# Both half-step ffns of a hybrid diffusion layer: from three token blocks to two token halves, with seven block products for gate, up and down

## The chip, the cores and the metric

One NeuronCore of a Trainium2 chip runs the whole kernel. The metric is the device time of one execution in microseconds; the kernel before takes 2794.5 us, the median of three runs (2792.1 to 2797.2). PE is TensorE, DVE VectorE, ACT ScalarE, POOL GpSimd; SP is the engine whose queue issues most DMAs.

## The reference

One layer for 1024 latent and 128 prompt tokens, each kind with its own conditioning vector. The change concerns the two ffns:

```
m = silu(cvec) @ ada_w + ada_b          # nine vectors of 1024: shift, scale, gate for three steps
x += 1/2 * gate1 * swiglu(modulate(rms_norm(x, ffn1_norm), shift1, scale1), w_gu, w_down)
x += gate2 * merge(attention A, attention B)
x += 1/2 * gate3 * swiglu(modulate(rms_norm(x, ffn2_norm), shift3, scale3), w_gu, w_down)
y = rms_norm(x, final_norm)
swiglu(h) = (silu(a) * u) @ w_down,   [a, u] = h @ w_gu
```

The model width is 1024, the hidden width 2816, all in float32.

## The kernel before

Activations lie transposed: width on 128 partitions times KD = 8, tokens along the row. The T = 1152 tokens make three blocks of BW = 384. The hidden width makes NF = 22 units j of 128; unit j has 128 gate and 128 up columns. Every float32 operand is split into a high and a low part (`split`: ACT casts, L175; DVE or POOL subtracts, L176), and one product of float32 is three matmuls (`mm3`: high weight by high activation L204, high by low L205, low by high L206). Weights come by DMA into `raw` and are split into `whi` and `wlo`.

Gate and up of an ordinary block take 2 x 8 x 3 = 48 matmuls per unit (`gu`). Blocks 1 and 2 are taken as a pair (`gu_pair`, L519): the two blocks by two halves of the width are a 2 by 2 matrix of activations, gate and up by two halves of the width a 2 by 2 matrix of weights, and their product is formed by seven block products with sums and differences in place of eight. `norm_pair` (L467) builds the sums of activations (tiles t0 to t2), POOL four combinations of the weights per unit (L543). That makes 48 + 84 = 132 matmuls of 384 columns per unit. Down (`down`, L437) is plain, in groups of two or three units, 22 x 8 x 3 x 3 = 1584 matmuls, each result scaled and added to x by DVE (`upd`, L414). Hidden activations stay in SBUF.

What follows in PE's stream is the order in which generators yield: the main program (`ffn`, L596) runs, and at every yield `step` lets side jobs take turns at a rate of so many per yield (`spawn`). Side jobs are the normalizations (`self.cm`), and the rest of the modulation vectors (`ada_rest`, L767, rates AR = (2, 0.4)): the first two are made before anything else (L747), the other seven in four groups as matmuls of 512 columns (L256) among the products. `need_gate` and `finish` run a side job to its end where its result is needed. A tile's buffer is filled again only when its last reader is done, and each engine runs its instructions in order, as does SP its DMAs.

## Time and profile before

| | |
|---|---|
| median of 3 runs | 2794.5 us |
| the profiled execution | 2805.29 us, 10.8 above the median |
| its span, first to last instruction | 2803.2 us |
| mean granted clock of TensorE | 0.979 |
| instructions | 39143 |
| DMA | 290.46 MB, mean 104 GB/s |

A row of the page or of a view names a line, an engine, an operation, the tile written and the tiles read, with shapes (partitions x columns); busy is the time of such instructions, and idle before is time in which their engine had nothing to do just ahead of them, with what ended it. The busy time of PE counts a stretch of overlapping matmuls once, so the distance between matmuls is read from starts, or from a count in a stretch that is busy throughout.

### The profile page before, as it was taken

To read this page: it belongs to the slowest core of one execution; us is meant where nothing else is said; L and a number is where in the kernel's file an instruction comes from. 1 tells how busy PE (TensorE), PEld (TensorE's weight loads), DVE (VectorE), ACT (ScalarE), POOL (GpSimd) and SP (SyncE) were. 2 spreads that over 40 slices of the span, in tenths; PEclk is the share of its full clock that TensorE was granted. 3 is DMA by queue.
4 is the path that set the end of the run, shared out by engine and by line. 5 is a ranking of instruction groups with operands and counts; after the bars stand their busy time and mean duration, and the time that the engine had idled before them with its cause. 6 is when DMAs were issued, how large, how long until landed. Compare 5 with 4: busy or idle time off the path is not lost.

```text
span 2803.2 us, 39143 instructions
## 1 busy us (share of the span) xinstructions
PE 2684.7 (96%) x15049; PEld 2505.1 (89%) x15049; DVE 1811.5 (65%) x2867; ACT 1049.0 (37%) x1636; POOL 762.0 (27%) x523
## 2 busy tenths in 40 slices
PE   7899999999999998899999989899999999999998
PEld 5699999999999998788877777789999999999998
DVE  3765555555687656566677777557676655555676
ACT  4522222222344533355555455235542222222333
POOL 2421111111233101244345444233331111111232
PEclk9999999999999999899999999999999999999997
DMA  7543332111214465433323233684421111111213
GB/s 264 173 130 104 108 111 83 46 46 46 99 45 158 139 206 164 112 86 90 91 72 102 77 97 116 192 281 150 128 78 44 45 46 46 46 46 46 76 53 106
DMA packets 161968, 290.46 MB, mean 104 GB/s; under 512 B 20206, under 2 KB 114914, under 8 KB 158454
## 3 DMA queue, kind: packets, MB, share of 16 engines
q1 hardware_dynamic: 160054, 283.24, 32.1%
q10 hardware_dynamic: 1728, 4.72, 0.4%
q8 instruction: 119, 1.95, 0.3%
q14 instruction: 67, 0.55, 0.1%
HBM read 233.77 MB, written 53.99 MB: 103 GB/s over the span
## 4 chain that ended last, share of the span: by engine, by line
PE 45%; DVE 6%; ACT 4%; issue 2%; DMA 2%; POOL 1%; SPq 0%; DVEq 0%; ACTq 0%; POOLq 0%
PE ps_g L206 7%; PE ps_g L204 7%; PE ps_g L205 7%; PE pp_m L205 3%; PE pp_m L204 3%; PE pp_m L206 3%; DVE pl L1298 3%; PE pp_o L204 1%; PE pp_o L205 1%; PE pp_o L206 1%; ACT ph L1297 1%; PE pp_o L1242 1%; ACT pf L1296 1%; PE pp_m L1213 1%; PE pp_o L1241 1%
## 5 line engine op out<-in xcount | busy, mean ns | idle before, releaser
L204 PE MATMUL ps_g<-hh,whi 128*128 128x384 f32 x1284 | 437.7, 342 | 11.7 <-ACT whi L175 6.1
L206 PE MATMUL ps_g<-hh,wlo 128*128 128x384 f32 x1284 | 436.3, 340 | 5.8 <-DVE wlo L176 5.8
L205 PE MATMUL ps_g<-hl,whi 128*128 128x384 f32 x1284 | 436.6, 340 | 1.8 <-DVE hl L176 1.8
L543 POOL TENSOR_TENSOR adaw<-adaw 128x512 f32<-128x512 f32 x132 | 181.7, 1376 | 813.3 <-DVE wlo L176 784.2
L176 DVE TENSOR_TENSOR wlo<-raw,whi 128x1024 fp32r<-128x1024 f32 (+1 forms) x203 | 261.5, 1289 | 167.3 <-ACT whi L175 167.0
L175 ACT CAST whi<-raw 128x1024 fp32r<-128x1024 f32 (+1 forms) x203 | 209.5, 1033 | 400.0 <-PE ps_g L205 215.1
L1305 POOL TENSOR_TENSOR acc<-acc,pf 128x1024 f32<-128x1024 f32 (+3 forms) x128 | 235.1, 1842 | 378.3 <-ACT pf L1296 271.6
L175 ACT CAST whi<-adaw 128x1024 fp32r<-128x1024 f32 x132 | 138.9, 1052 | 449.4 <-PE ps_g L205 310.4
L204 PEld LDWEIGHTS ps_g<-hh,whi 128*128 128x128 f32 x1284 | 245.4, 191 | 19.2 <-ACT whi L175 7.4
L206 PEld LDWEIGHTS ps_g<-hh,wlo 128*128 128x128 f32 x1284 | 245.4, 191 | 12.2 <-DVE wlo L176 9.1
L205 PEld LDWEIGHTS ps_g<-hl,whi 128*128 128x128 f32 x1284 | 245.8, 191 | 6.6 <-DVE hl L176 3.0
L204 PE MATMUL pp_m<-hh,whi 128*128 128x384 f32 x732 | 249.0, 340 | 1.8 <-ACT whi L175 1.3
L205 PE MATMUL pp_m<-hl,whi 128*128 128x384 f32 x732 | 249.8, 341 | 0.0
L206 PE MATMUL pp_m<-hh,wlo 128*128 128x384 f32 x732 | 249.1, 341 | 0.0
L176 DVE TENSOR_TENSOR wlo<-adaw,whi 128x1024 fp32r<-128x1024 f32 x132 | 170.4, 1291 | 106.2 <-ACT whi L175 105.9
L206 PE MATMUL ps_g<-ah,wlo 128*128 128x384 f32 x682 | 229.9, 337 | 2.3 <-DVE wlo L176 2.3
L204 PE MATMUL ps_g<-ah,whi 128*128 128x384 f32 x682 | 231.2, 339 | 0.0
L205 PE MATMUL ps_g<-al,whi 128*128 128x384 f32 x682 | 229.6, 337 | 0.0
L1298 DVE TENSOR_TENSOR pl<-pf,ph 128x1024 fp32r<-128x1024 f32 (+1 forms) x96 | 170.4, 1779 | 68.2 <-ACT ph L1297 65.9
L414 DVE SCALAR_TENSOR_TENSOR y<-ps_g,gate,y 128x384 f32<-128x384 f32 (+2 forms) x271 | 127.2, 503 | 42.4 <-PE ps_g L206 42.0
L204 PEld LDWEIGHTS pp_m<-hh,whi 128*128 128x128 f32 x732 | 139.4, 190 | 8.5 <-ACT whi L175 1.6
L205 PEld LDWEIGHTS pp_m<-hl,whi 128*128 128x128 f32 x732 | 139.5, 191 | 7.2 <-issue 2.7
(486 smaller groups left out, 6180.4 us busy)
## 6 DMA issues: line engine op xcount, KB each, us to landing
adaw<-gu SPq DMA_DIRECT2D x66, 512.0 KB
raw<-wd SPq DMA_DIRECT2D x52, 512.0 KB
adaw<-ada_w SPq DMA_DIRECT2D x24, 1024.0 KB
raw<-gu SPq DMA_DIRECT2D x46, 512.0 KB
raw<-win SPq DMA_DIRECT2D x27, 512.0 KB
raw<-wout SPq DMA_DIRECT2D x24, 512.0 KB
raw<-wo SPq DMA_DIRECT2D x16, 512.0 KB
gate_sp<-tmp SPq DMA_DIRECT2D x41, 192.0 KB
```

Of the source, the lines that this page charges most:

```text
L175: self.nc.scalar.copy(hi, src)
L176: (eng or self.nc.vector).tensor_sub(lo, src, hi.bitcast(F32))
L204: nc.tensor.matmul(ps, wh[:, c], mh, start=(start and i == 0), stop=False)
L205: nc.tensor.matmul(ps, wh[:, c], ml, start=False, stop=False)
L206: self.mm = nc.tensor.matmul(ps, wl[:, c], mh, start=False, stop=(stop and i == n - 1))
L414: nc.vector.scalar_tensor_tensor(x[:, d, c0:c1], ps[:, c0:c1], gate[:, d, c:c + 1], x[:, d, c0:c1], op0=ALU.mult, op1=ALU.add)
L543: nc.gpsimd.tensor_tensor(o, x, y, op=op)
L1213: nc.tensor.matmul(ps, q1[0:96, t * P:(t + 1) * P], k1[0:96, c0:c1], start=True, stop=True)
L1241: nc.tensor.matmul(out, V(kt), ph[:, i, :q1 - q0], start=(first[hf] == (n, i)), stop=False)
L1242: nc.tensor.matmul(out, V(kt), pl[:, i, :q1 - q0], start=False, stop=end)
L1298: nc.vector.tensor_sub(pl, pf, ph.bitcast(F32))
L1305: nc.gpsimd.tensor_add(av[:, :m, a0:a0 + w], av[:, :m, a0:a0 + w], pf[:, i:i + m, :])
```

## The change

The three blocks go, in the ffns. The tokens make two halves of HF = 576, each two units U = 288 of PSUM width. Seven planes of activations (A11, A12, A22, S, T0, T1, T2; four slices of 128 rows, high and low) hold the entries, sums and differences of the 2 by 2 matrix, now over all tokens, and both gate and up (`hidden`) and down (`down`) are seven products: 7 x 2 x 12 = 168 matmuls of 288 columns per unit, 3696 in all, and 1848 for down.

- `first` and `lead`: while the second half of x is on its way, the products with A11 and A12 of the gate run for the first seven units (SOLO); their results go to DRAM (st_sp) and come back in `hidden`.
- `half0` and `half1` modulate the halves and build the planes; `half1` is a side job that `ffn` finishes ahead of unit 0.
- `hidden` stores activations in DRAM (act_sp).
- `down` goes over three chunks of 8, 8 and 6 units; a ring of three slots holds the planes, rebuilt for each chunk from act_sp. Accumulators u2 and v collect products in SBUF over the chunks; in the last chunk they are combined and added to y (L693 to L697). x comes into y by 32 DMAs on POOL's queue in the two ffns, which add in place (`addx`).
- `ada` makes one vector at a time, through the eight buffers r that also hold x and later act_sp; AR is 0.42, and `ffn1` finishes that side job ahead of down.
- The normalization ahead of the attention and the last one read y in the new pieces (`hook`).

Its core, with what is removed cut short:

```diff
-    def gu_pair(self, wgu, j, rest, end=False):
...
-    def down(self, wd, js, blocks, gate, stats=False):
...
+AR = 0.42
+CM = (3, 1.5)
...
+    def ada(self, m):
...
+        for k in range(KD):
+            raw = self.Rp.tile([P, T], F32, name="r", bufs=KD)[:, :D]
+            nc.sync.dma_start(raw, a["ada_w"][k * P:(k + 1) * P, m * D:(m + 1) * D])
+            yield
+            for cg in range(4):
+                nc.tensor.matmul(ps[32 * cg:32 * cg + 32, :256], self.cs[:, k, :],
+                                 raw[:, cg * 256:(cg + 1) * 256], start=(k == 0), stop=(k == KD - 1))
+            yield
+        pv = self.turned(ps)
...
+    def half1(self, i):
...
+        for k in range(4):
+            self.modulate(i, k, 1, rs, False)
+            self.modulate(i, 4 + k, 1, rs, True)
+            yield
+            a, b = self.xk[k], self.xk[4 + k]
+            a0, a1, b0, b1 = a[:, :HF], a[:, HF:], b[:, :HF], b[:, HF:]
+            V.tensor_sub(a0, a1, a0)
+            self.plane("A22", k, b1, G)
+            G.tensor_sub(a1, b1, a1)
+            self.plane("S", k, a0)
+            yield
+            self.cross(k, a0, b0, b1, V, G)
+            self.plane("T1", k, a1, G)
+            yield
+            self.plane("T2", k, b0)
+            yield
...
+    def cross(self, k, a0, b0, b1, e0, e1):
...
+            e0.tensor_sub(t, b1[:, u], a0[:, u])
+            self.split(hi[:, k, u], lo[:, k, u], t)
+            e1.tensor_sub(b0[:, u], b0[:, u], t)
...
+    def hidden(self, wgu, j, led):
...
+        W = self.wsplit(ru[:, 512:], 512)
         for o, x, y, op in ((ru[:, 512:], ru[:, :512], ru[:, 512:], ALU.add),
...
             nc.gpsimd.tensor_tensor(o, x, y, op=op)
...
+        SG = self.wsplit(rg)
+        u2 = [self.rtile()[:, :U] for _ in range(2)]
+        for ci in range(2):
+            b6 = self.bank()
+            self.prod(b6, SG, 0, 4, "T0", ci)
+            nc.vector.tensor_add(u2[ci], b6, c1[ci])
+        yield
+        SU = self.wsplit(ru)
+        for ci in range(2):
+            b7 = self.bank()
+            self.prod(b7, SU, 0, 4, "T1", ci)
...
+            self.prod(d, W, 0, 4, "T2", ci)
...
+            nc.sync.dma_start(self.act_sp[:, j, U * ci:U * ci + U], up)
...
+            self.prod(c, SU, 4, 4, "S", ci)
...
+            self.prod(g, SG, 4, 4, "A22", ci)
...
+    def down(self, wd, gate, xsrc, rp, up, order, hook):
...
+                nc.sync.dma_start(ra[i], self.act_sp[:, f0 + i, :])
+            for n in ("A11", "A12", "T1", "T0", "T2", "S", "A22"):
+                self.pl[n] = slot()
...
+        def addx(ds, half):
+            for d in ds:
+                h = slice(HF * half, HF * half + HF)
+                nc.gpsimd.dma_start(y[d][:, h], xsrc[:, d, h], accum_op=ALU.add)
...
+            if last:
+                for k in range(4):
+                    V.tensor_add(v[:, k, :], v[:, k, :], u2[:, k, :])
+                    for d, c0, s in ((4 + k, 0, v), (4 + k, HF, v), (k, HF, u2)):
+                        for e0, e1, m in parts(c0, c0 + HF):
+                            V.scalar_tensor_tensor(y[d][:, e0:e1], s[:, k, e0 - c0:e1 - c0], gate[:, d, m:m + 1],
+                                                   y[d][:, e0:e1], op0=ALU.mult, op1=ALU.add)
+            for q in range(2):
+                w = self.wsplit(raw[q, 3], n)
+                for dd, ci in pl:
+                    p = self.bank()
+                    self.prod(p, w, dd * kc, kc, "T2", ci)
+                    out(c, 4 + 2 * q + dd, U * ci, p)
...
+    def ffn(self, n, wgu, j0=0):
+
+        for j in range(j0, SOLO[n]):
+            yield from self.lead(wgu, [j])
+        self.finish(self.cm)
+        self.after_cm()
+        for j in range(NF):
+            yield from self.hidden(wgu, j, j < SOLO[n])
...
+        yield from self.ffn(0, self.a["gu1"], 2)
+        self.finish(self.ar)
```

How the order of instructions moves, at three places. A row names line, operation, tile written and tiles read, its shape, and xN for N alike in a row.

The modulation vectors of ffn1, on PE and SP (cs is the conditioning vector, ident a unit matrix for transposes, al and ah activations). PE before, in the midst of down's products:

```order
L204 MATMUL ps_g<-ah,whi 128x384
L205 MATMUL ps_g<-al,whi 128x384
L206 MATMUL ps_g<-ah,wlo 128x384
L256 MATMUL pp_m<-adaw,cs 32x512 x4
L204 MATMUL ps_g<-ah,whi 128x384
```

PE now, at the end of gate and up (A22 of the last unit) and the start of down (n0 is the ring's first slot):

```order
L205 MATMUL ps_g<-A22l,whi 128x288
L206 MATMUL ps_g<-A22h,wlo 128x288
L275 MATMUL pp_m<-ident,tmp 128x128 x2
L250 MATMUL pp_m<-r,cs 32x256 x32
L275 MATMUL pp_m<-ident,tmp 128x128 x2
...
L250 MATMUL pp_m<-r,cs 32x256 x32
L275 MATMUL pp_m<-ident,tmp 128x128 x2
L204 MATMUL ps_g<-n0h,whi 128x288 x2
L204 MATMUL pp_m<-n0h,whi 128x288
```

SP's DMAs now, at the same place:

```order
L551 DMA act_sp<-tmp 128x288 x2
L247 DMA r<-ada_w 128x1024
L646 DMA ry<-wd 128x2x512
L568 DMA act_sp<-tmp 128x288 x2
L247 DMA r<-ada_w 128x1024 x24
L593 DMA r<-act_sp 128x1152 x8
L646 DMA ry<-wd 128x2x512 x3
```

Four of the seven vectors have moved behind the last product of gate and up, and 24 of their loads stand ahead of those of act_sp.

The start of ffn1 on POOL (x and r hold x; ac, ca sums of squares; hl, t1l, A22l and T1l remainders; raw weights of a unit). Before:

```order
L348 TENSOR_TENSOR ca<-ca,tmp 128x384 x14
L480 TENSOR_TENSOR ca<-x_109,cb 128x384
L176 TENSOR_TENSOR hl_751<-ca,hh_750 128x384
L480 TENSOR_TENSOR tmp<-x_110,bc 128x384
L176 TENSOR_TENSOR hl_753<-tmp,hh_752 128x384
L176 TENSOR_TENSOR t1l<-tmp,t1h 128x384
...
L176 TENSOR_TENSOR hl_753<-tmp,hh_752 128x384
L543 TENSOR_TENSOR raw<-raw 128x512 x3
L176 TENSOR_TENSOR t1l<-tmp,t1h 128x384
L543 TENSOR_TENSOR raw<-raw 128x512 x33
L543 TENSOR_TENSOR adaw<-adaw 128x512 x32
```

Now:

```order
L325 TENSOR_TENSOR ac<-ac,tmp 128x288 x14
L418 TENSOR_TENSOR r<-r,bc 128x288 x4
L418 TENSOR_TENSOR r<-r,cb 128x288 x4
L447 TENSOR_TENSOR r<-r 128x576
L176 TENSOR_TENSOR A22l<-r,A22h 128x576
L464 TENSOR_TENSOR r<-r,tmp 128x288 x2
L176 TENSOR_TENSOR T1l<-r,T1h 128x576
...
L464 TENSOR_TENSOR r<-r,tmp 128x288 x2
L176 TENSOR_TENSOR T1l<-r,T1h 128x576
L531 TENSOR_TENSOR raw<-raw 128x512 x4
L531 TENSOR_TENSOR rx<-rx 128x512 x4
```

In both, the combinations of weights stand behind the planes; what changed is the width of a row, and that four combinations are now needed by the first unit after the lead.

The last chunk of down on DVE (u_6424 is u2; n2l a plane's remainder; rx weights). Before, in down's products:

```order
L414 SCALAR_TENSOR_TENSOR x_109<-ps_g,gate_90,x_109 128x384
L176 TENSOR_TENSOR wlo<-adaw,whi 128x1024
L414 SCALAR_TENSOR_TENSOR x_110<-ps_g,gate_90,x_110 128x256
L414 SCALAR_TENSOR_TENSOR x_110<-ps_g,gate_90,x_110 128x128
L414 SCALAR_TENSOR_TENSOR x_109<-ps_g,gate_90,x_109 128x384
```

Now, between T0's last addition and T2's weight remainder:

```order
L621 TENSOR_TENSOR u_6424<-u_6424,ps_g 128x288
L696 SCALAR_TENSOR_TENSOR y<-u_6424,gate_94,y 128x128
L693 TENSOR_TENSOR v<-v,u_6424 128x576
L176 TENSOR_TENSOR n2l<-r,n2h 128x576 x3
...
L693 TENSOR_TENSOR v<-v,u_6424 128x576
L696 SCALAR_TENSOR_TENSOR y<-u_6424,gate_94,y 128x448
L696 SCALAR_TENSOR_TENSOR y<-v,gate_94,y 128x576
L696 SCALAR_TENSOR_TENSOR y<-v,gate_94,y 128x448
L696 SCALAR_TENSOR_TENSOR y<-v,gate_94,y 128x128
L696 SCALAR_TENSOR_TENSOR y<-u_6424,gate_94,y 128x128
L176 TENSOR_TENSOR wlo<-rx,whi 128x768
```

The additions that went along with each product now stand together ahead of a weight remainder (`wlo`).

## Rows read from the trace of the kernel before

**Rows 1.** The page's head: span, then each engine's busy us (share) xinstructions.

```profile
span 2803.2 us, 39143 instructions
PE 2684.7 (96%) x15049; PEld 2505.1 (89%) x15049; DVE 1811.5 (65%) x2867; ACT 1049.0 (37%) x1636; POOL 762.0 (27%) x523
```

**Rows 2.** Busy time by stretch: stretch, its us, busy us of each engine, clock, DMA.

```profile
core 0: us, PE busy (x) PEld busy (x) DVE busy (x) ACT busy (x) POOL busy (x), PEclk, DMA share, GB/s
0.00:50.00 50.00, 33.31 (x216) 20.64 (x216) 13.44 (x28) 15.27 (x25) 10.86 (x13) 0.93 0.80 286
50.00:200.00 150.00, 137.28 (x734) 119.08 (x732) 98.97 (x138) 72.64 (x123) 56.27 (x42) 0.94 0.48 159
200.00:800.00 600.00, 598.93 (x3477) 578.64 (x3476) 362.82 (x603) 151.97 (x214) 100.91 (x75) 1.00 0.25 81
1900.00:2100.00 200.00, 196.41 (x1133) 195.28 (x1132) 141.14 (x197) 97.20 (x156) 70.89 (x53) 0.99 0.37 117
2100.00:2600.00 500.00, 500.00 (x2887) 500.00 (x2886) 296.42 (x479) 120.82 (x170) 75.74 (x56) 1.00 0.15 47
```

**Rows 3.** Timeline of PE at 1368 us: start, duration, line; 256-column matmuls.

```profile
1368.00 0.28 PE L1416 MATMUL ps_S<-q,k 128*128 128x256 f32 x1
1368.12 0.28 PE L1417 MATMUL ps_S<-q,k 66*128 66x256 f32 x1
1368.24 0.28 PE L1420 MATMUL ps_S<-bandT,identr 128*128 128x256 f32 x1
1368.36 0.34 PE L204 MATMUL pp_m<-hh,whi 128*128 128x384 f32 x1
```

**Rows 4.** Busy time by stretch, line L747 (first two modulations) alone.

```profile
0.00:50.00 50.00, 13.75 (x128) 3.33 (x128) 0.93 0.80 286
```

**Rows 5.** Timeline of POOL around 71 to 83 us: start, busy us, line.

```profile
71.60 6.64 POOL L348 TENSOR_TENSOR ca<-ca,tmp 128x384 f32<-128x384 f32 x5 [4.38 <-ACT tmp L347]
82.16 1.88 POOL L480 TENSOR_TENSOR ca<-x,cb 128x384 f32<-128x384 f32 x1 [3.92 <-issue]
```

**Rows 6.** Busy time by stretch as in rows 2, the first 40 us.

```profile
10.00:20.00 10.00, 2.89 (x20) 1.75 (x22) 0.03 (x1) 5.00 (x10) 6.95 (x7) 1.00 1.05 378
20.00:30.00 10.00, 7.17 (x51) 3.45 (x43) 4.86 (x11) 2.90 (x5) 1.60 (x1) 0.91 0.98 353
30.00:40.00 10.00, 10.00 (x59) 6.87 (x59) 5.67 (x8) 4.71 (x7) 2.09 (x1) 0.75 0.83 279
```

**Rows 7.** Groups of POOL's instructions by line and shape: xcount | busy us, mean ns.

```profile
L543 POOL TENSOR_TENSOR adaw<-adaw 128x512 f32<-128x512 f32 x132 | 181.7, 1376 | 813.3 <-DVE wlo L176 784.2 <-DVE var L310 21.3
L1305 POOL TENSOR_TENSOR acc<-acc,pf 128x1024 f32<-128x1024 f32 x64 | 160.0, 2500 | 210.6 <-ACT pf L1296 177.5 <-DVE pl L1298 22.8 <-ACT nm L1140 9.7
L348 POOL TENSOR_TENSOR ca<-ca,tmp 128x384 f32<-128x384 f32 x43 | 54.3, 1265 | 125.8 <-ACT tmp L347 123.7 <-DVE y L414 0.4
L1305 POOL TENSOR_TENSOR acc<-acc,pf 128x256 f32<-128x256 f32 x16 | 12.2, 764 | 139.4 <-ACT pf L1296 67.5 <-DVE pl L1298 59.5 <-DVE mx L1188 7.3
```

**Rows 8.** Groups of DVE's instructions by line and shape, columns as in rows 7.

```profile
L176 DVE TENSOR_TENSOR wlo<-raw,whi 128x1024 fp32r<-128x1024 f32 x187 | 245.3, 1312 | 155.8 <-ACT whi L175 155.5
L1298 DVE TENSOR_TENSOR pl<-pf,ph 128x1024 fp32r<-128x1024 f32 x64 | 123.6, 1935 | 38.3 <-ACT ph L1297 38.3
L1298 DVE TENSOR_TENSOR pl<-acc,ph 128x1024 fp32r<-128x1024 f32 x32 | 39.0, 1219 | 25.6 <-ACT ph L1297 25.6
L414 DVE SCALAR_TENSOR_TENSOR y<-ps_g,gate,y 128x384 f32<-128x384 f32 x123 | 73.8, 613 | 18.5 <-PE ps_g L206 18.5
L583 DVE TENSOR_TENSOR tmp<-tmp,cc 128x384 f32<-128x384 f32 x44 | 44.0, 1000 | 1.5
L592 DVE TENSOR_TENSOR ca<-ca,cb 128x384 f32<-128x384 f32 x44 | 24.6, 558 | 0.0
L176 DVE TENSOR_TENSOR wlo<-raw,whi 128x768 fp32r<-128x768 f32 x16 | 16.3, 1017 | 11.5 <-ACT whi L175 11.5
L414 DVE SCALAR_TENSOR_TENSOR y<-ps_g,gate,y 128x128 f32<-128x128 f32 x74 | 25.3, 342 | 0.0
```

**Rows 9.** Busy time by stretch, line L256 (the other seven modulations) alone.

```profile
50.00:500.00 450.00, 34.85 (x224) 4.97 (x224) 0.98 0.37 122
```

**Rows 10.** The page's groups: one of PE's weight loads.

```profile
L204 PEld LDWEIGHTS ps_g<-hh,whi 128*128 128x128 f32 x1284 | 245.4, 191 | 19.2 <-ACT whi L175 7.4
```

More of the change, by code (lines that the diff above doesn't have):

```diff
@@ new lines, in planes, with plane_tiles, plane, modulate @@
+    def planes(self, name, ns):
+        self.plp = self.pool(name)
+        self.plane_tiles(ns)
+    def plane_tiles(self, ns):
+        for n in ns:
+            self.pl[n] = tuple(self.plp.tile([P, 4, HF], F32R, name=n + c) for c in "hl")
+    def plane(self, n, i, src, eng=None):
+        hi, lo = self.pl[n]
+        self.split(hi[:, i, :], lo[:, i, :], src, eng)
+    def modulate(self, i, k, half, rs, flip):
+        nc = self.nc
+        x = self.xk[k]
+        for ci, r in enumerate(rs):
+            c0 = HF * half + U * ci
+            (nc.gpsimd if flip else nc.vector).tensor_mul(x[:, c0:c0 + U], x[:, c0:c0 + U], r)
+        for c0, c1, c in parts(HF * half, HF * half + HF):
+            G, sh = self.G[i][:, k, c:c + 1], self.mod(3 * i)[:, k, c:c + 1]
+            if flip:
+                nc.vector.tensor_scalar(x[:, c0:c1], x[:, c0:c1], G, sh, op0=ALU.mult, op1=ALU.add)
+            else:
+                nc.scalar.activation(x[:, c0:c1], x[:, c0:c1], AF.Identity, scale=G, bias=sh)
@@ L767, in ada_rest @@
-    def ada_rest(self):
-        for g in range(1, 5):
-            yield from self.ada(g)
-            self.ada_done = g
-            self.ar[1] = AR[1]
-        self.room = 1
-    def need_gate(self):
-        while self.ada_done < 1:
-            next(self.ar[0])
+            if n == 6:
+                for u in range(2):
+                    for _ in self.inv(U * u, U):
+                        pass
+                rs = [self.spread(U * u, U) for u in range(2)]
+            if n == 7:
+                ws = [self.wload(self.a["gu1"][0, 0], 1024)]
@@ new lines, in ffn1, with rest, hook @@
+        yield from self.down(self.a["wd1"], self.gate[0], self.a["xT"], rp, up, (2, 1, 0), hook)
+    def ffn2(self):
+        self.close("mg")
+        self.wx = self.pool("wx2", side="right")
+        PA = self.plp
+        self.plp = self.pool("PB")
+        def rest():
+            yield from self.inv(2 * BW, BW)
+            self.plane_tiles(PLANES[4:])
+            yield from self.half1(2)
+        self.finish(self.cm)
+        self.cm = self.spawn(rest(), CM[1])
+        self.after_cm = lambda: None
+        yield from self.ffn(1, self.a["gu2"])
+        self.close("PB", "PA")
+        rp = self.pool("ring2")
+        up = self.pool("uv2")
+        yp = self.pool("y2")
+        self.yk = [yp.tile([P, T], F32, name="y", bufs=KD) for _ in range(KD)]
+        def hook(i):
+            if i == 0:
+                g = self.final((0, 1), HF)
+                next(g)
+                next(g)
+                self.spawn(g, FR)
+            else:
+                for u in (2, 3):
+                    g = self.final((u,), U)
+                    next(g)
+                    self.spawn(g, FR)
+        yield from self.down(self.a["wd2"], self.gate[2], self.x2_sp, rp, up, (0, 1, 2), hook)
@@ L1543, in merge @@
             yield
+        self.xk = [rt() for _ in range(KD)]
         nx = gated(1)
@@ L1548, in merge, with lead @@
                 nx = gated(b + 1)
+            if b == 2:
+                self.close("h", "h0")
+                self.planes("PA", PLANES[:4])
+                def lead():
+                    yield from self.inv(BW, BW)
+                    rs = [self.spread(U * u, U) for u in range(2)]
+                    yield
+                    yield from self.half0(2, range(KD), rs)
+                self.cm = self.spawn(lead(), CM[1])
             for d in range(KD):
```

936 lines of the change are left out of this document (447 added, 489 removed).

## The prediction, made before the changed kernel had run

> **What bounds the kernel now.** I read the page's head first: TensorE (PE) is busy 2684.7 of 2803.2 us, VectorE (DVE) 65%, GpSimd (POOL) 27% [rows 1]. Then the busy time in stretches, since the shares average over stages with different limits [rows 2]. In both half-step ffns PE never stops: 598.93 of 600 us in the first one's body, 500.00 of 500 in the second's. Of the idle time, 16.69 us lie in the first 50 us and 12.72 in the next 150 (the row's 150 less 137.28), 29.4 together, while inputs arrive and the normalized blocks are built. So the ffns have one currency, PE time, and the other engines work beside it: DVE at 296.42 of 500 us, POOL at 75.74. A change that cuts PE work gains in full only if it opens no gap in PE's stream.
>
> The profiled execution took 2805.3 us, 10.8 above the median of 2794.5. I make the sum against the former and take 10.8 off at the end.
>
> **PE work.** The old matmul: 2887 in 500 us, all busy, is 0.1732 us each for 384 columns [rows 2]. One of 288 columns does not occur. The nearest are those of 256: three start-to-start intervals make 0.36 us, each matmul with a weight load of its own [rows 3]. On the line through both, 288 columns cost 0.120 + 32/128 x 0.0532 = 0.1333 us. Both ffns had 2 x (22 x 132 + 1584) = 8976 matmuls: 1554.6 us. Now each has 3696 for gate and up (22 x 7 products x 24) and 1848 for down, 11088 in all: 1478.1 us. Difference **-76.5 us**. Ends: in proportion to columns (0.1299 each) -114; with the starts' rounding (0.37 us for the three, so 0.1358 for 288) -49.
>
> The Trainium skill, "TensorE: Matmul & The Clock Gate", section "Back-to-back issue gap", gives N/2.4 GHz plus about 2.5 ns: 162.5 ns for 384 columns and 122.5 for 288, so -101 us by the rule at both ends. The rows lie 11 to 13 ns above it.
>
> **Start of ffn1: +32.** Before hidden unit 0 can go through its other five products, planes S, A22, T0, T1 and T2 must stand. They come from half1, which needs the second half of x. Until then PE has the two leading products of seven units: 7 x 2 x 2 x 12 = 336 matmuls x 0.1333 = 44.8 us, plus the first modulations, 13.75 us [rows 4]; nothing else. When does it get on? In the old kernel POOL summed the squares of the later blocks until 78 us and began its modulation at 82 [rows 5]. Now the second half of x is asked for behind the first leading pass. I put half1's start at 64: x asked for at about 40 us, 2.36 MB at 353 GB/s [rows 6] 7 us, fourteen sums of squares at about 0.9 us, some 4 us for root and spreading. half1 itself, per k of four: POOL has four operations of 288 and three of 576. From POOL's rows [rows 7], between 764 ns (256) and 1265 (384) lies 0.89 for 288, and between 1376 (512) and 2500 (1024) 1.52 for 576: 32.4 us for all four k. DVE has six of 288 and three of 576, all with two SBUF operands: between 558 (384) and 1017 (768) [rows 8] that is 0.44 and 0.79, 20.1 us in all.
>
> Do the two run side by side? The rows say no: the same 384-column product of two SBUF tiles takes 558 ns at L592 and 1000 at L583, and the same 1024-column subtraction 1219 or 1935 [rows 8]. So I add them and, since POOL's means already hold some of that waiting, take 50 us out of 52.5. The ends are 32 (full overlap) and 55.
>
> Behind half1, POOL still makes the four weight combinations of unit 0 (4 x 1.376 = 5.5), then a cast (about 1) and wlo (1.3): the body begins at 64 + 50 + 7.5 = 121.5. PE has done 58.5 us of work by then and lost 63; the old loss was 29.4. That is +32 rounded down for work I may have missed, with ends +12 and +45.
>
> **Boundary in ffn1: +27.** Seven modulation vectors used to be spread over the gate and up products. With AR = 0.42 their 125 or so steps get 52 turns, so the order shows three of seven done there and four, 32 of 56 loads of 512 KB, behind the last A22 product and ahead of down's first. One vector's eight buffers are loaded ahead; the other 24 loads (12.58 MB) and the four activation rows that the first plane needs (2.36 MB) wait for PE to free those buffers. The DMA engines moved 378 GB/s at the most in the rows I have [rows 6], so 39.5 us, and with the first landing and the first plane's split some 45. PE's own work in that time is 4/7 of 34.85 = 19.9 us [rows 9], which was paid before too. Net +25, and +2 since behind the loads of the start PE's granted clock was 0.75, half of that stretch at the lower of its two levels [rows 6]. Ends: +14 and +40.
>
> **Down: +19.5 and +18.** One chunk product stage takes PE 12.8 us (96 matmuls), in the last chunk 9.6 (72). The first two chunks give DVE 72 to 81 us and PE 89.6: covered. In the last, ahead of T2's wlo, DVE has 22 rows left when T0 ends: four plane remainders, sums and scaled additions over 576 or 448+128 columns. With 0.34 for 128 and 0.82 for 576 by the line through 342 and 613 ns [rows 8], they come to 13.7 us, wlo 1.0. PE can run the high parts of six products meanwhile (36 x 0.1333 = 4.8): a gap of 9.9. Then S and A22 cost DVE 18.8 us of scaled additions and splits beside some 8 of the next normalization, against 19.2: +7.5. The earlier stages lose 2. Ends 10 and 35 each; ffn2 has the same order, with a little less behind it.
>
> **The two other joints: +6 and +16.5.** The normalization of blocks 1 and 2 now starts only when down ends, with one block (12.5 us of PE) ready: +6 (2 to 10). ffn2's lead has the same 44.8 us of PE work against 7.5 + 50 + 7.5 = 65 for half1 and the first combinations; the old loss there was 3.6 us [rows 2]: +16.5 (0 to 28).
>
> **Costed at nothing.** The stores and loads of activations (2 x 12.98 MB each way) lie beside PE streams that use DMA at a share of 0.15 [rows 2]. If that cover fails, it is at ffn2's boundary, where rows of units 0 to 7 were stored long before. The body: per unit DVE has 12.5 us and POOL four combinations, 5.5, against 22.4 of PE. The 32 accumulating DMAs on POOL's queue have no row; POOL has 60 of 89.6 us free in chunk 0, so 16 of them cost nothing up to 3.7 us each. I take nothing, since the nearest POOL row of that size is 1.5.
>
> **Sum:** -76.5 + 32 + 27 + 19.5 + 18 + 6 + 16.5 = +42.5. 2805.3 + 42.5 - 10.8 = **2837 us**, 1.5% slower.
>
> **Rivals.**
> - *DVE and POOL run beside each other (faster).* Then each half1 takes 32 us. Start: body at 103.5, loss 45, +15.5. ffn2's lead: 47 against 44.8, about 0. Last chunk: additions shrink by the share that waited, +12 and +11; joint +3. With +27 at the boundary 68.5, less 76.5: -8, or **2786**. With the rule's or the column price of 288, or without the boundary's wait, 2750 to 2765. It decides once half1 takes less than about 38 us. For it: POOL's means hold waits already, L592 shows DVE undisturbed. Against: L583 and L1298. Chance 0.25.
> - *The accumulating DMAs hold POOL up.* At 6 us each, 16 x 2.3 = 37 us past the cover in each ffn: +74, **2911**. For it: POOL's plane subtractions stand behind them in its order. Against: chunk 1 needs the sum in y only late. Chance 0.08. The Trainium skill, "SBUF — State Buffer", section "SBUF: two separate sides", says that POOL itself writes the descriptors of such a DMA and is locked out while DVE holds their common port, so that one of 620 ns alone took some 3100. By that figure 16 would fill 50 of the 60 us, and the sum stays; no row here shows such a DMA.
> - *The 288-column matmul is no faster than its weight load.* A load takes 191 ns [rows 10]; at 0.1732 as before, 11088 cost 1920 us, +366, **3280**. Against: 256 columns at 0.12 with a load each. Chance 0.02.
>
> **Numbers.** Forecast case 0.65. Its unknowns (-114 to -49 for PE, gaps from 48 at all lower ends to 193 at all upper ones) don't all fall one way; I let it reach from 2790 to 2880. The range takes the faster rival's main part too: 2765 to 2885. A measurement here can tell 0.2%, 5.6 us. Faster: the first rival's 0.25 less its edge, and the forecast's lower tail, 0.26. Same: 0.08. Slower: 0.66.
>
> **What would show it.** Matmuls of 288 columns every 0.133 us; PE idle of about 63 us in the first 125; one stretch of some 45 us with PE on the vectors and DMA near its full rate between gate/up and down; gaps of about 10 us at T2 in the last chunk, released by wlo; and 15 to 20 us at the start of ffn2. A start without a wait for POOL's T1 and combinations would make the prediction wrong, and so would down stages that wait for planes in every chunk.

## The result and the profile after

The changed kernel takes 2963.7 us (median of four runs, 2960.7 to 2968.2) against 2795.9 for the kernel before (four runs): a ratio of 1.060 [1.058, 1.063]. The forecast was 2837, in a range from 2765 to 2885: the sign was right, the size was not. The profiled executions, 2960.7 and 2805.3 us, differ by 155; on that basis the sum had said 42.5.

The page's head after, beside [rows 1]:

```profile
span 2958.5 us, 45764 instructions
PE 2656.4 (90%) x17389; PEld 2461.7 (83%) x17389; DVE 1902.1 (64%) x3044; ACT 1102.2 (37%) x1880; POOL 1058.8 (36%) x753
```

PE's busy time fell by only 28 us, its idle time rose from 118.5 to 302.1. Busy time by stretch, as in [rows 2], after:

```profile
core 0: us, PE busy (x) PEld busy (x) DVE busy (x) ACT busy (x) POOL busy (x), PEclk, DMA share, GB/s
0.00:135.00 135.00, 74.55 (x516) 61.57 (x516) 71.06 (x103) 67.65 (x129) 73.04 (x72) 0.83 0.61 208
300.00:618.00 318.00, 318.00 (x2435) 308.53 (x2434) 167.58 (x308) 79.88 (x137) 72.32 (x54) 1.00 0.31 98
618.00:658.00 40.00, 29.22 (x272) 8.66 (x270) 6.72 (x17) 1.92 (x4) 1.65 (x1) 0.70 0.97 378
658.00:962.00 304.00, 264.17 (x1869) 259.27 (x1868) 259.31 (x372) 123.74 (x224) 150.21 (x106) 0.93 0.34 99
962.00:2087.00 1125.00, 1033.70 (x5571) 904.56 (x5570) 744.23 (x1161) 521.84 (x848) 395.75 (x248) 0.97 0.44 134
2087.00:2157.00 70.00, 54.25 (x360) 52.75 (x358) 53.34 (x66) 34.56 (x69) 46.87 (x34) 0.89 0.38 121
2300.00:2633.00 333.00, 333.00 (x2502) 331.77 (x2501) 177.95 (x327) 90.86 (x156) 78.57 (x60) 1.00 0.26 80
2633.00:2958.00 325.00, 268.31 (x1900) 263.50 (x1898) 267.79 (x399) 124.77 (x232) 162.49 (x123) 0.91 0.30 84
2500.00:2550.00 50.00, 50.00 (x377) 49.84 (x377) 24.80 (x45) 13.62 (x24) 13.39 (x11) 1.00 0.22 70
```

The stretches are, in order: to the first product with T0, gate and up without a lead, the modulation vectors, down, the mix (attention and merge), ffn2's lead, its gate and up, its down, and a piece of it. Gate and up run without a gap, 377 matmuls in 50 us: 0.1326 us each, where 0.1333 was forecast. The loss lies elsewhere: in ffn1's down PE has 40 us of idle time, and DVE is busy for 259 of 304 us. Before, the mix took 1094 us and ffn2 818, with DVE at 64% of ffn2:

```profile
891.00:1985.00 1094.00, 1025.70 (x5556) 900.86 (x5555) 736.29 (x1146) 516.60 (x842) 391.80 (x240) 0.98 0.44 134
1985.00:2803.00 818.00, 801.56 (x4578) 798.47 (x4577) 526.50 (x831) 251.21 (x372) 171.09 (x129) 0.98 0.19 61
```

So ffn1 grew by 71 us (from 891 to 962), the mix by 31 and ffn2 by 53. In the table "lost" is elapsed time less what the stretch's products need back to back at full rate: down of ffn1, from 658.5 to 961.8, is 303.3 - 1848 x 0.1326 = 58. It holds idle time (40 us there) and the slower matmuls behind it.

| part | forecast | measured |
|---|---|---|
| matmuls of both ffns, by counts and intervals | -76.5 | -84 (11088 x 0.1326 less 1554.6) |
| PE idle before the first product with T0 | 63, at 121.5 us | 60.7, at 135.3 us |
| lost in the seven led units, ffn1 and ffn2 | 0 and 0 | 24 and 29 |
| boundary of ffn1, elapsed | 45 | 40 |
| lost in down up to its last product, ffn1 and ffn2 | 19.5 and 18 | 58 and 62 |
| mix, longer by | 6 | 31 |
| lost in ffn2's lead | 20 | 25 |

The led units are counted from their first T0 product to that of the first unit without a lead (135.3 to 277.2, 2157.1 to 2304.0); 4.5 of the 24 us are matmuls of the modulation vectors. The measured entries are losses of the changed kernel, not differences, so they add up to more than 155: the kernel before lost time too. Elapsed time less the products and the vectors' matmuls (13.75 and 34.85 us, [rows 4] and [rows 9]) was 65 us in ffn1 and 41 in ffn2, and is 178 and 136 now; with -84 for the products and +31 for the mix that is the whole 155.

Five places in PE's timeline after (start, duration, line, and in brackets the idle time before it with what ended it):

```profile
135.26 0.61 PE L204 MATMUL pp_m<-T0h,whi 128*128 128x288 f32 x1 [27.72 <-ACT whi L175]
193.53 0.40 PE L204 MATMUL pp_m<-T0h,whi 128*128 128x288 f32 x1 [1.12 <-ACT whi L175]
902.88 0.61 PE L204 MATMUL pp_o<-n1h,whi 128*128 128x288 f32 x1 [7.94 <-DVE v L621]
928.65 0.61 PE L206 MATMUL ps_g<-n0h,wlo 128*128 128x288 f32 x1 [11.77 <-DVE wlo L176]
2905.96 0.61 PE L206 MATMUL pp_o<-n0h,wlo 128*128 128x288 f32 x1 [11.81 <-DVE wlo L176]
```

The gap at T2 of the last chunk, 11.8 us ahead of wlo in both ffns, is the one forecast (9.9). The others in ffn1's down were not: 7.94 us at T0 of that chunk, and 5.21, 3.29, 3.00, 2.05 and 1.98 us in the first two, all released by DVE.

### The profile page after: what moved, and what is told of

It is laid out like the page before. It is cut to its first block, busy times and chain, and to the rows that moved or that the text cites. A ratio compares the mean times of both kernels' runs of the same rounds, so it can differ in the third digit from the quotient of the medians.

```text
span 2958.5 us, 45764 instructions
## 1 busy us (share of the span) xinstructions
PE 2656.4 (90%) x17389; PEld 2461.7 (83%) x17389; DVE 1902.1 (64%) x3044; ACT 1102.2 (37%) x1880; POOL 1058.8 (36%) x753
## 5 line engine op out<-in xcount | busy, mean ns | idle before, releaser
L175 ACT CAST whi<-raw 128x1024 fp32r<-128x1024 f32 (+2 forms) x191 | 188.2, 986 | 486.9 <-issue 170.9
L176 DVE TENSOR_TENSOR wlo<-raw,whi 128x1024 fp32r<-128x1024 f32 (+2 forms) x191 | 230.7, 1209 | 187.4 <-ACT whi L175 184.5
L531 POOL TENSOR_TENSOR rx<-rx 128x512 f32<-128x512 f32 x88 | 115.9, 1317 | 371.0 <-DVE wlo L176 365.8
L531 POOL TENSOR_TENSOR raw<-raw 128x512 f32<-128x512 f32 x88 | 115.6, 1314 | 336.4 <-DVE wlo L176 331.2
L176 DVE TENSOR_TENSOR wlo<-rx,whi 128x1024 fp32r<-128x1024 f32 (+2 forms) x94 | 102.2, 1087 | 116.7 <-ACT whi L175 115.9
L204 PE MATMUL ps_g<-hh,whi 128*128 128x384 f32 x344 | 119.8, 349 | 14.8 <-ACT whi L175 13.0
L206 PE MATMUL ps_g<-hh,wlo 128*128 128x384 f32 x344 | 118.4, 345 | 3.1 <-DVE wlo L176 3.1
L1314 DVE TENSOR_REDUCE mxB<-pp_m 128x1 f32<-128x512 f32 (+1 forms) x192 | 107.0, 592 | 20.5 <-PE pp_m L1313 19.5
L1342 PE MATMUL pp_o<-pl,v 128*128 128x512 f32 (+2 forms) x272 | 105.0, 387 | 15.6 <-DVE pl L1398 15.5
L205 PE MATMUL ps_g<-hl,whi 128*128 128x384 f32 x344 | 118.9, 346 | 0.0
```

The lines of the kernel that those rows point to most:

```text
L175: self.nc.scalar.copy(hi, src)
L176: (eng or self.nc.vector).tensor_sub(lo, src, hi.bitcast(F32))
L204: nc.tensor.matmul(ps, wh[:, c], mh, start=(start and i == 0), stop=False)
L205: nc.tensor.matmul(ps, wh[:, c], ml, start=False, stop=False)
L206: self.mm = nc.tensor.matmul(ps, wl[:, c], mh, start=False, stop=(stop and i == n - 1))
L531: nc.gpsimd.tensor_tensor(o, x, y, op=op)
```

## The experiments

Each kernel ran once with a profile, beside the kernel before on the same chip (2790.5 to 2794.2 us, medians where it ran more often); the two complete versions and the last one ran four or five times. The changed kernel is 2963.7 throughout. All edits are to it. The mix took 1119 to 1126 us in all runs with seven products in down, though most edits leave it alone; differences of a few us between single runs are therefore not read. ffn1's down is timed to its last product, ffn2's to PE's last matmul, which adds some 6 us of the last normalization.

### Down: who holds DVE up

**Theory A:** DVE's two-input SBUF operations and POOL's sums block each other, so DVE becomes down's bound in every chunk. **Rival B:** only the order of the last chunk costs, where the remainder for T2 stands behind the additions.

The first run leaves POOL's sums out of both downs: the differences of activations for T1 and T2 and the sums of weights.

```diff
-            e1.tensor_sub(b0[:, u], b0[:, u], t)
+            if e1 is not None:
+                e1.tensor_sub(b0[:, u], b0[:, u], t)
...
-                        G.tensor_sub(a0, a1, a0)
-                        G.tensor_sub(a1, b1, a1)
+                        pass
...
-                        self.cross(i, a0, b0, b1, V, G)
+                        self.cross(i, a0, b0, b1, V, None)
...
-                G.tensor_sub(raw[q, 0], raw[q, 0], raw[q, 2])
...
-                G.tensor_sub(raw[q, 0], raw[q, 3], raw[q, 0])
-                G.tensor_add(raw[q, 2], raw[q, 2], raw[q, 3])
...
-                G.tensor_sub(raw[q, 1], raw[q, 1], raw[q, 0])
```

> This kernel leaves out, in both down stages, every sum that POOL makes: the differences of activation rows for planes T1 and T2 and the weight combinations. All matmuls, all splits and all additions of results stay. Theory A (in down, DVE and POOL block each other's operations on two SBUF tiles, and this makes DVE the bound): the mean of DVE's plane remainders of 576 columns falls from 1.03 to 1.20 us to about 0.76, that of the 288-column difference at L462 from 1.17 to about 0.45; DVE is busy some 205 us in ffn1's down instead of 259; the down stage of ffn1 (304 us, of which 245.5 are PE work) shrinks to 255 to 270, leaving only the wait ahead of T2's weight remainder in the last chunk; the whole falls from 2964 to 2880 to 2900. Theory B (DVE's own work and its order are too much for the stage, POOL has little to do with it): the stage stays above 290 us and the whole within 20 us of 2964.

Measured: 2886.5 us; ffn1's down took 263.2 instead of 303.3, ffn2's 275.5 instead of 313.7. DVE's groups in that stretch (xcount | busy us, mean ns | idle before), first in the changed kernel:

```profile
L176 DVE TENSOR_TENSOR n0l<-r,n0h 128x576 fp32r<-128x576 f32 x22 | 21.8, 1031 | 1.5 <-ACT n0h L175 1.4
L176 DVE TENSOR_TENSOR n1l<-r,n1h 128x576 fp32r<-128x576 f32 x22 | 25.3, 1196 | 0.2
L176 DVE TENSOR_TENSOR n0l<-tmp,n0h 128x288 fp32r<-128x288 f32 x8 | 12.4, 1574 | 0.0
L462 DVE TENSOR_TENSOR tmp<-r 128x288 f32<-128x288 f32 x22 | 25.1, 1168 | 3.3 <-POOL ac L325 3.3
L615 DVE SCALAR_TENSOR_TENSOR y<-ps_g,gate,y 128x288 f32<-128x288 f32 x56 | 27.5, 508 | 7.4 <-PE ps_g L206 7.4
```

and in the run without the sums:

```profile
L176 DVE TENSOR_TENSOR n0l<-r,n0h 128x576 fp32r<-128x576 f32 x22 | 15.6, 752 | 0.2
L176 DVE TENSOR_TENSOR n1l<-r,n1h 128x576 fp32r<-128x576 f32 x22 | 15.4, 751 | 2.2 <-ACT n1h L175 2.2
L176 DVE TENSOR_TENSOR n0l<-tmp,n0h 128x288 fp32r<-128x288 f32 x8 | 3.4, 451 | 0.0
L462 DVE TENSOR_TENSOR tmp<-r 128x288 f32<-128x288 f32 x22 | 10.2, 488 | 3.4 <-DMA r<-act_sp 3.4
L615 DVE SCALAR_TENSOR_TENSOR y<-ps_g,gate,y 128x288 f32<-128x288 f32 x56 | 27.9, 512 | 11.9 <-PE ps_g L206 11.9
```

The counts are equal. Each of these subtractions of two SBUF tiles is 1.4 to 3.5 times as long while POOL makes its sums; the addition that reads PSUM (L615) is not (508 and 512 ns). DVE's busy time in the stretch falls from 259 to 198 us. That DVE merely waited for POOL's results doesn't fit: in the changed kernel 3.7 of its 44.6 us of idle time in this stretch are ended by POOL, and none of PE's gaps above 0.7 us is. Without the sums down loses 263.2 - 245.0 = 18 us, near the 19.5 forecast, and of PE's gaps only the one at T2 is left (11.77 us). The Trainium skill, "SBUF — State Buffer", section "SBUF: two separate sides", says that a DVE instruction with two SBUF inputs and a GpSimd one that reads SBUF take a common port pair in turn, each for its whole length; these rows agree as far as they go, since they show longer operations and not the port.

The second run moves the sums of activations from POOL to DVE, which takes work from POOL and gives it to the bound engine:

```diff
-                        G.tensor_sub(a0, a1, a0)
-                        G.tensor_sub(a1, b1, a1)
+                        V.tensor_sub(a0, a1, a0)
+                        V.tensor_sub(a1, b1, a1)
...
-                        self.cross(i, a0, b0, b1, V, G)
+                        self.cross(i, a0, b0, b1, V, V)
```

> The activation sums of down (T1's two differences, T2's) move from POOL to DVE; the weight combinations stay on POOL. Theory A: DVE gets 27 us more work per ffn, but its operations lose less to POOL than that: L462 from 1.17 to about 0.5 us, plane remainders from 1.1 to about 0.9; DVE's busy time in the stage falls from 259 to about 235, the stage from 304 to about 280, the whole to about 2915. Theory B: DVE's busy time rises by about 27 us, each down stage is 15 to 27 us longer, the whole 2995 to 3015.

Measured: 2930.1; down 289.4 and 296.1. Though DVE does more, down is 14 and 18 us shorter, if less so than expected. DVE has 416 operations in the stretch where it had 372, and is busy for 245 us instead of 259:

```profile
660.00:949.00 289.00, 257.87 (x1866) 254.45 (x1865) 245.08 (x416) 122.14 (x224) 90.87 (x61) 0.95 0.35 103
```

The third tests B: in the last chunk the remainders for T2's weights are made ahead of the additions.

```diff
+            w3 = [self.wsplit(raw[q, 3], n) for q in range(2)]
             if last:
...
-                w = self.wsplit(raw[q, 3], n)
+                w = w3[q]
```

> Only the order in the last chunk of down changes: T2's two weight tiles are split ahead of the 22 additions that stood before the remainder. If the wait of 11.8 us at T2 is this order, it goes, in both ffns: 20 to 28 us less, about 2940. If DVE's backlog is what counts, the same work is then waited for at the next results that T2 hands to DVE (PSUM tiles run out): waits of 6 to 12 us stay in the same 30 us, and the whole changes by less than 10 us.

Measured: 2963.8, down 304.9 and about 319. Nothing is gained: what is taken from the gap at T2 is lost at the next places that wait for DVE (behind the start of T2 in ffn1, PE's largest gap is now 7.89 us, ended by L615), since DVE's backlog stays. In this kernel B is worth nothing by itself; what the new order would give without POOL's sums was not tried.

The fourth does down as eight plain products over the same halves: 2112 matmuls per ffn in place of 1848, four planes, no sums, no u2 and v.

```diff
-            for n in ("A11", "A12", "T1", "T0", "T2", "S", "A22"):
...
+            for half in range(2):
+                for q in range(2):
+                    for e in range(2):
+                        w0, w1 = self.wsplit(raw[q, 2 * e], n), self.wsplit(raw[q, 2 * e + 1], n)
...
+                                for kh, w in enumerate((w0, w1)):
+                                    hi, lo = self.pl[2 * half + kh]
+                                    self.mm3(p, w, range(kc), lambda i: (hi[:, i, u], lo[:, i, u]), w0=dd * kc,
+                                             start=kh == 0, stop=kh == 1)
...
```

> Down goes back to eight plain products over the two halves, from the activations in DRAM, gate and up keep their seven. PE work per ffn rises from 245 to 280 us (2112 matmuls of 288 columns at 0.1325), POOL has no sums to make and DVE's work falls to some 130 us in a stage. If down's gaps are DVE's and POOL's, the stage takes 282 to 292 us instead of 304 in ffn1 and 285 to 300 instead of about 325 in ffn2, with no wait over 2 us inside, and the whole is 2900 to 2930, faster than with seven products. If they are DMA's (activation rows that come late), the gaps stay and the whole rises to 3010 or more.

Measured: 2895.3, 68 us less than with seven products. Down by stretch in the run without sums, then here; and the first 55 us of the mix, here, in the changed kernel and in the kernel before, in this order:

```profile
663.00:926.00 263.00, 249.72 (x1867) 248.31 (x1867) 198.46 (x370) 122.37 (x223) 36.24 (x40) 0.98 0.38 113
```

```profile
658.00:944.00 286.00, 285.41 (x2136) 284.46 (x2137) 125.00 (x191) 108.53 (x179) 39.70 (x45) 0.99 0.37 110
943.70:998.70 55.00, 50.30 (x290) 49.12 (x289) 36.91 (x72) 30.31 (x62) 9.87 (x10) 0.97 0.37 124
```

```profile
961.80:1016.80 55.00, 45.21 (x242) 43.05 (x241) 35.76 (x71) 29.16 (x59) 13.28 (x13) 0.88 0.38 127
```

```profile
890.80:945.80 55.00, 52.69 (x298) 52.05 (x297) 38.61 (x76) 30.71 (x60) 14.45 (x13) 0.97 0.48 159
```

Plain down is bound by PE again (285.41 of 286 us busy) and beats seven products by 18 and 17 us in the stage. Seven products without any sums took 263: what they save on PE, some 22 us, the sums more than take back. The mix is 28 us shorter too, 1097.1 against 1125.4 (1095 to 1097 in all three runs with plain down). DVE's backlog is not the reason for that part: without POOL's sums the mix still took 1124. The likely reason, which no run changes alone, is the order of seven products, which completes blocks 1 and 2 only with the last product: in its first 55 us the mix gets 242 matmuls out, with plain down 290, before 298. That is some 10 us. The other 18 appear by the start of the attention, where PE waits 4.4, 5.7 and 5.3 us for the first loads, a maximum and a sum, with plain down once, 6.0 us (before, 4.1 and 6.8 us); what makes those late was not tried.

### The start, the boundary and the led units

The rate of the modulation vectors, so that all seven are done within gate and up:

```diff
-AR = 0.42
+AR = 1.1
```

> AR is 1.1 in place of 0.42, so that all seven modulation vectors are made among the gate and up products of ffn1. In the changed kernel 39.8 us lie between the last A22 product and the first product of down, with DMA at 409 GB/s and 24 loads in the way. If those loads, asked for late, are the whole of it, the joint falls to under 3 us, gate and up grow only by PE's own work on four vectors (15 to 20 us), and the whole falls by 20 to 25, to about 2940. If instead the loads stall PE wherever they stand, gate and up grow by 35 us or more and the whole does not change by more than 6.

Measured: 2948.3. The boundary went from 40.1 us to 1.2, but gate and up, with its lead, from 580.8 to 601.6, since the vectors' matmuls are paid there: 15 us gained. The boundary's cause was as forecast.

The second half of x asked for ahead of the lead:

```diff
-            for k in range(KD):
-                nc.sync.dma_start(self.xk[k][:, HF:], self.a["xT"][:, k, HF:])
...
+        for k in range(KD):
+            nc.sync.dma_start(self.xk[k][:, HF:], self.a["xT"][:, k, HF:])
```

> The eight loads of the second half of x are asked for ahead of the first leading pass, not behind its stores on SP's queue. In the changed kernel they were issued at 51.3 us, half1 began at 83 and unit 0's T0 product at 135.3. If the start is the chain x, squares, half1, the body begins 10 to 15 us earlier (120 to 125) and the whole falls by as much. If the loads only push back the modulation weights and gate weights that share the DMA engines, the lead starts later and the body begins within 4 us of 135.

Measured: 2963.7, the first T0 product at 135.01. A miss: the loads were not what half1 waited for. ACT's squares stand behind the results of the leading products, and the matmul that sums them (L336) stands late in PE's order, at 74 us in both.

A22 ahead of S in each unit, which frees the buffer of the summed gate weights (SG) earlier:

```diff
+        for ci in range(2):
+            g = self.bank()
+            self.prod(g, SG, 4, 4, "A22", ci)
...
-        for ci, up in enumerate(ups):
-            g = self.bank()
-            self.prod(g, SG, 4, 4, "A22", ci)
```

> In each hidden unit the product with A22 comes ahead of that with S. Weight tile SG is then read last one product (3.2 us) before the unit ends, so the next unit's SG can be cast in its buffer in time. If the 1.1 and 1.7 us ahead of each led unit's T0 product are that buffer, they go: the led units take 16.5 to 18 us instead of 18.9 in ffn1 and 20.4 in ffn2, and the whole falls by 20 to 30 us. If the cast waits for POOL's combinations, units stay as long as they are (within 0.5 us).

Measured: 2960.8, led units still 18.8 to 20.5 us apart, but for the first in ffn2 (21.9, before 21.7). SG's buffer is not what they wait for.

half1's sums and remainders wholly on DVE (the eight multiplications of L418 that POOL makes, 7.3 us, stay there, so fewer operations move than the expectation says):

```diff
-        V, G = nc.vector, nc.gpsimd
+        V, G = nc.vector, nc.vector
```

> half1's POOL operations (16 of 288 columns, 12 of 576) go to DVE. Measured, half1 took 43.5 us with both engines. If the two block each other (DVE alone: 20.1 + 16.5 = 37 us, and no waiting), half1 takes 35 to 39 us, the body of ffn1 begins at 127 to 131 instead of 135.3, ffn2's likewise, the whole falls by 8 to 16 us. If they do overlap in the main, DVE's added 16.5 us come out as half1 of 48 us or more, and the whole rises by 5 to 20.

Measured: 2946.2; the first T0 product, from this run's timeline of PE:

```profile
126.81 0.61 PE L204 MATMUL pp_m<-T0h,whi 128*128 128x288 f32 x1 [27.44 <-ACT whi L175]
```

It comes 8.5 us earlier though one engine does what two shared: half1's sums on both engines gain nothing from the second. DVE's subtraction of two 288-column tiles (L462) takes 1252 ns there in the changed kernel and 454 in this run, the remainder for S 1347 and 754. In the changed kernel POOL began half1 at 83.3 (L418) and the combinations at 128.9:

```profile
83.31 1.06 POOL L418 TENSOR_TENSOR r<-r,bc 128x288 f32<-128x288 f32 x1 [9.55 <-ACT bc L352]
...
128.85 5.28 POOL L531 TENSOR_TENSOR raw<-raw 128x512 f32<-128x512 f32 x4 [2.04 <-DVE wlo L176]
```

The led units. In the changed kernel, T2 of one unit ends at 205.7; the timelines of ACT, DVE and POOL then show the chain to the next unit's T0 product at 213.88:

```profile
205.79 0.62 ACT L175 CAST whi<-raw 128x512 fp32r<-128x512 f32 x1 [8.93 <-issue]
...
206.45 0.69 DVE L176 TENSOR_TENSOR wlo<-raw,whi 128x512 fp32r<-128x512 f32 x1
...
207.22 5.53 POOL L531 TENSOR_TENSOR raw<-raw 128x512 f32<-128x512 f32 x4 [14.82 <-DVE wlo L176]
...
212.78 1.04 ACT L175 CAST whi<-raw 128x1024 fp32r<-128x1024 f32 x1 [6.37 <-POOL raw L531]
```

The cast of W gets its buffer when T2 is done. W, its remainder, POOL's four combinations and the cast of SG take 8.2 us one after another, while PE has S and A22, 6.4 us, and after a 1.1-us gap it runs slower for a while in some units. Units without a lead hide the chain behind the products with A11 and A12. The test makes T2 the first product of a unit (ACT copies its result, DVE adds it later):

```diff
         W = self.wsplit(ru[:, 512:], 512)
+        ds = []
+        for ci in range(2):
+            d = self.bank()
+            self.prod(d, W, 0, 4, "T2", ci)
+            up = self.tmp(U)
+            nc.scalar.copy(up, d)
+            ds.append(up)
+        yield
...
-            self.prod(d, W, 0, 4, "T2", ci)
...
+            up = ds[ci]
+            nc.vector.tensor_add(up, up, c1[ci])
```

> In each hidden unit the product with T2 comes first and its result is set aside by ACT. The rows of the changed kernel show, in a led unit, the chain: T2's last matmul, cast of W (its buffer is free only then), W's remainder, four combinations on POOL (5.5 us), cast of SG, next unit: 8.2 us, against 6.4 us of PE in the two products S and A22 behind T2. If this chain makes the led units 18.9 and 20.4 us long (15.9 of work), they come down to 16 to 16.7 us with T2 ahead, seven in each ffn: 40 to 60 us less, about 2910. If something else ends last (DMA of the weights, DVE), they stay above 18 us and the whole within 10 us of 2964.

Measured: 2902.6, 61 us less. Led units are 15.90 us apart in ffn2, which is their matmuls' own time (120 x 0.1326 = 15.9), and 16.67 in ffn1, where each also holds eight matmuls of the vectors. Gate and up fall from 580.8 to 559.6 us in ffn1 and from 476.0 to 445.3 in ffn2 (there without the lead), 52 us of the 61. A stretch of 40 us within them, here and then in the changed kernel:

```profile
160.00:200.00 40.00, 40.00 (x312) 38.29 (x310) 27.24 (x50) 10.51 (x17) 10.91 (x9) 1.00 0.54 163
```

```profile
160.00:200.00 40.00, 36.31 (x265) 34.56 (x264) 20.66 (x42) 6.78 (x10) 10.60 (x8) 0.96 0.51 161
```

The second half of x first, with its squares ahead of the lead too:

```diff
+        for k in range(KD):
+            for u in (2, 3):
+                self.stat(k, U * u, U)
...
-            for k in range(KD):
-                for u in (2, 3):
-                    self.stat(k, U * u, U)
-                yield
```

> As e2, with the squares of x's second half also put ahead of the leading products. In e2 x arrived earlier, but ACT squared it only behind the leading results, half1 began at 83 as before and nothing was gained. If the start is bound by this order, half1 begins at 62 to 72 us, unit 0's T0 product at 114 to 126 instead of 135, and the whole falls by 9 to 20. If half1 is bound by DVE's and POOL's work beside the leading products, it begins earlier and takes longer, and the body starts within 5 us of 135.

Measured: 2970.1; half1 began at 79 instead of 83 but took 47 us on POOL instead of 43.5, and the first T0 product came at 135.42. A miss again: the squares now delay the modulations of the first half on ACT, and L336 stays at 73.5 us in PE's order.

Ten units led instead of seven, to fill PE's wait:

```diff
-SOLO = (7, 7)
+SOLO = (10, 10)
```

> SOLO is (10, 10) in place of (7, 7): three more units have their two leading products made ahead of half1's end, 19 us of PE work. If PE lacks work there, the gap of 27.7 us ahead of unit 0 shrinks to about 9 to 14, gate and up end 10 to 19 us earlier in ffn1 (less 3 units that become led units of 18.9 us with their own gap, +2.5 us each), ffn2 gains 0 to 8, the whole falls by 5 to 15. If DVE sets the end, unit 0's T0 product moves from 135 to 141 or later by what the three units cost DVE (some 6 us), the gap stays above 18 us, and the whole is level or longer.

Measured: 2988.2, a miss with the wrong sign.

```profile
144.71 0.40 PE L204 MATMUL pp_m<-T0h,whi 128*128 128x288 f32 x1 [3.49 <-ACT whi L175]
```

The gap of 27.7 us shrinks to 3.5, but three more units then pay for the chain above, and T0 starts 9 us later.

### Whole versions

Plain down with T2 first, half1 on DVE, AR = 1.3 and x with its squares first; beside it the same with seven products in down, their sums on DVE.

> Together: plain down, T2 first, AR 1.3, half1's sums on DVE, x and squares first; gate and up keep their seven products. The single gains (68 of plain down, 15 of AR, 17 of half1, 40 to 60 of T2 first, 0 to 15 of the start) leave 2964 at 2790 to 2830. If the seven products of gate and up pay at all (13 us of PE time per ffn), this ends level with the kernel before or within 35 us above it.

Measured: 2817.0 (2814.6 to 2819.0), 1.009 [1.007, 1.010] of before.

> As f3, but down with its seven products and its activation sums on DVE. In d2 that down took 289 and 296 us, plain down in d4 285 and 297. If this holds beside the other edits, and the mixing stage loses 26 us to DVE's backlog as in d2, it takes 15 to 40 us more than f3.

Measured: 2842.9 (2839.8 to 2843.9), 1.018 [1.016, 1.019]. The downs now tie (286 and 294 us with seven products, 285 and 294 with eight), and the 26 us between the two lie in the mix, 1124.6 against 1095.3. So seven products in down win nothing even with the sums of activations on DVE. The sums of weights are still POOL's there, and L462 takes 904 ns, for 488 without any sums; seven products with no sum on POOL were not tried.

Plain down as above, ten led units in both ffns, x in the order of the change:

> Plain down, T2 first, AR 1.3, half1's sums on DVE and ten leading units in both ffns (x loaded as in the changed kernel). Against f3's 2817: if PE lacks work in the lead, 8 to 25 us less, 2792 to 2809, at or just above the kernel before; if DVE sets the end there, 2810 to 2825. Below 2790 would say that seven products of gate and up pay over halves after all.

Measured: 2808.2 (2806.3 to 2810.4), 1.006 [1.004, 1.008]. That is 8.8 us less than with seven led units. The order of x differs too, but loading x first had gained nothing by itself; with T2 first, ten led units seem to help. No version of these beats the kernel before.

## Why the prediction was right or wrong

**PE work: right.** -76.5 was forecast, -84 measured; the line through 256 and 384 columns [rows 2, 3] gave 0.1333 for 0.1326. The rival of weight loads falls. Two figures beside it were slips: 162.5 and 122.5 ns make -100 us, not -101, and the rows lie about 11 ns above such values, not 11 to 13.

**Start of ffn1: right in size, partly by luck.** PE was idle for 60.7 us; less the old 29.4 [rows 2] that is 31 for a term of +32. But the first T0 product came 13.8 us later than forecast, since PE was busy for 74.5 us ahead of it, not 58.5 (granted clock 0.83, and small matmuls of the normalizations). half1 began at 83, not 64: the terms left out ACT's and PE's order ahead of the sums, which the two misses with x showed, and x was asked for at 51.3, not 40. Against that it took 43.5 us on POOL (83.3 to 126.8), not 50, though its sum for DVE had left out the eight scalings of L422 (4.3 us). That DVE and POOL don't run freely side by side in it was shown by moving the sums to DVE.

**Boundary: right.** 40 us for 45, with DMA at 409 to 411 GB/s from 628 to 658 us, above the 378 of [rows 6]; the run with AR = 1.1 removed it. Net of the vectors' own 19.9 us that is 20, for +27; by that run, which paid them in gate and up, it is 18.

**"The first two chunks give DVE 72 to 81 us and PE 89.6: covered": wrong, the largest error.** DVE's and POOL's collisions, read from [rows 8] and used for half1, were not applied to down. DVE's operations were priced alone (0.79 for 576 columns; 0.75 measured alone), but took 1.03 to 1.20 beside POOL, and up to 1.57 in place of 0.45 for 288. Cover of 9 to 18 us per chunk was gone, and PE lost 58 and 62 us for 19.5 and 18. Some 18 of the 58 are not idle time but, in the main, matmuls at a lower rate: the granted clock is 0.93 and 0.91 in the two downs, 1.00 in gate and up. The forecast gap at T2 was there, 11.8 for 9.9, and with POOL's sums left out the forecast loss was too, 18 us: the failed step is the price of DVE's operations beside POOL.

**"Costed at nothing: the body": wrong.** The 22.4 us of PE per unit are those of a unit without a lead; a led one has 15.9, and the chain from T2 to the next T0 stands in series in it. The order shows it; it was read for half1 alone. The run with T2 first gave back 21 and 31 us in gate and up, for the 24 and 29 lost in the led units.

**The joint: +6 forecast, +31 for the whole mix.** The first 55 us cost about 10, near the upper end given; the rest lies where no term looked, and which wait of the attention is late was not settled.

**ffn2's lead: near.** 25 lost for 20.

**The rivals.** That DVE and POOL run side by side is refuted by the groups above, and half1's 43.5 us lie above the 38 named for it; it would have been the case faster than before. The accumulating DMAs held nothing up: POOL's group in ffn1's down,

```profile
L626 POOL DMA_DIRECT2D y<-xT x16 | 15.4, 996 | 33.9 <-ACT y L613 25.9 <-ACT n1h L175 4.1 <-DVE y L615 3.5
```

about 1 us each, where 3.7 would still have been covered. By the 3100 ns that the Trainium skill gives ("SBUF — State Buffer", section "A bandwidth-pool intuition that's wrong (but worth ruling out)") for such a DMA under a DVE copy, sixteen would be an estimated 50 us. The row shows 15.4, but DVE ran no copy in that stretch, so it does not show the page's case.

**What no term but the boundary's held** is that PE runs slower behind some gaps. The products' work fell by 84 us and PE's busy time by 28, while the mean granted clock went from 0.979 to 0.949. How much of the loss would stay with the gaps but without the lower clock was not measured by itself.

## What to carry to other kernels

Seven block products for eight trade PE columns for subtractions and additions of SBUF tiles; price those in every stage at the durations they have beside POOL, and compare with the plain product, which here was the quicker down (286 us for 303, and for 263 if the sums had cost nothing). When a stage loses part of its matmuls, ask again which serial chain the removed ones had covered. Look at the order in which results become complete: a scheme that finishes everything with its last product takes the cover from the next stage.
